# State-space mixer with outputs made as [feature, token] and the norm's scale applied behind the out-projection

## The chip, the cores and the metric

The kernel runs on 1 of the 8 cores of one Trainium2 chip. Its engines work side by side, each on its own queue: TensorE (PE, with its weight loads as PEld), VectorE (DVE), ScalarE (ACT), GpSimd (POOL) and SyncE (SP), which issues most DMAs. The metric is the device time of one execution in microseconds (us), as the median of several runs.

## What is computed

A two-layer decoder trunk on 512 tokens of 1024 features in float32. Layer 0 mixes with attention, layer 1 with a state-space mixer; each layer is `x <- LN(alpha*x + mixer(x))`, then a feed-forward part with a norm of its own and a gated embedding. Only the mixer of layer 1 changes:

```python
def ssd_mixer(x, w_in, conv_w, conv_b, dt_bias, a_log, d_skip, norm_w, w_out):
    h = x @ w_in
    z, xbc, dt = split(h)                       # 2048, 3072, 32
    xbc = silu(causal_depthwise_conv(xbc))      # 4 taps
    xs, bm, cm = split(xbc)                     # 32 heads of 64; 4 groups of B and C, 128 states
    dt = softplus(dt + dt_bias); a = -exp(a_log)
    y = ssd_chunked_scan(xs, dt, a, bm, cm)     # chunks of 128 tokens:
    #   la = cumsum(dt*a);  xdt = xs*dt
    #   y  = (cb * exp(la_i - la_j), j <= i) @ xdt         "intra"
    #   y += (C @ state) * exp(la_i)                       "inter"
    #   state = state*exp(la_end) + B^T (exp(la_end - la) * xdt)
    y = y + d_skip*xs
    y = y * silu(z)
    y = y * rsqrt(mean(y*y over the group's 512 features) + eps) * norm_w
    return y @ w_out
```

## The kernel before, in words

Products of large operands are made of three matmuls each (`mm3`, L104 to L107): an operand is split into a high and a low part in fp32r (`split`, L71: ACT writes the high part at L73, DVE the low one at L76; weights with a gain go through L98 and L99), and high x high, high x low and low x high are added up in PSUM. Weight tiles come by DMA from SP's queue into `raw`, are split into the 10 tiles of `wp`, and so run ahead of PE. The small products of the scan are plain float32 matmuls; each shows in the trace as two matmul instructions.

`ssd` (L755) works group by group: 4 groups `g` of 8 heads (512 features), 4 chunks `c` of 128 tokens. `Inputs(g).part(0..3)` makes the group's inputs: part 0 B and C (`conv_in`: projection as [feature, token], convolution, SiLU; then `bk` turns B on PE), parts 1 and 2 the 512 features of x, two blocks of 128 each, turned to [token, feature] on PE (`xf`, L969, evacuated by ACT at L970), part 3 the gate z as [token, feature] (`proj_b`: four accumulators side by side, evacuated at L976 and L977 into four tiles `z`). `Scan.chunk(c)` makes the state (L904), `intra` (L914: for each head the weights E, 128x128, with 64 moving columns), `inter` (L918: one matmul of 512 columns), adds them to `y = d_skip * xf` (POOL, L899; DVE, L915 to L921), multiplies with z (L924), takes the sum of squares (ACT, L927), `rsqrt` (DVE L126, POOL L127) and scales y (L929). `turn` transposes y on PE (L936) and splits it into `yT`. `mixer_out` multiplies yT with the out-projection, whose weights carry `norm_w` as gain, and adds to the residual stream `xs` (L203, L205).

The loop at L986 runs the scan of group g with the parts of group g+1 and the out-projection of group g-1 between its chunks; the last group has no inputs to make, and `mixer_last` follows it with the layer norm. The order within each engine's queue is not written out here: a planner builds it from a simulated timeline, in which program order is the priority and the buffers of each pool (`one`, `two`, `three`, `four`, `zp`, `cvp`, `yp`: the number is that of their buffers) hold an instruction back until a tile is free. Each engine then runs its queue strictly in that order.

In the attention part, `values` (L363, L368) makes products with 64 columns of weights for two heads in turn, whose results go to partitions 0 to 63 and 64 to 127 of one accumulator; the change uses that form.

Of the kernel before, what the change touches and what calls it, by code (L numbers as in the profile page):

```python
# [33 lines left out]
def trunk(ctx, tc, I, out):  # L34
# [720 lines left out]
    def ssd(xs, xT):  # L755
        with ExitStack() as es:
# [7 lines left out]
            zp = lpool("zp", 4)  # L764
            cvp = lpool("cvp", 2)
            yp = lpool("yp", 3)
# [4 lines left out]
            gn = one.tile([P, 16], F32, name="gn")  # L771
            nc.scalar.dma_start(gn, I["ssd_norm"])
            hv = one.tile([P, 3, 32], F32, name="hv")
            nc.scalar.dma_start(hv, I["ssd_heads"].partition_broadcast(P))
            dtb, alog, dsk = hv[:, 0], hv[:, 1], hv[:, 2]
# [53 lines left out]
            ones = scr("ones")  # L829
            G.memset(ones[:, :P], 1.0)  # L830
            b2 = bank("le")
            T.matmul(b2[:, :P], ones[:, :P], da, start=True, stop=True)
            ela, eend, elast = (one.tile([P, P], F32, name=n) for n in ("ela", "eend", "elast"))
            A.activation(ela, la, AF.Exp)
# [3 lines left out]
            rows = dp.tile([P, P], F32, name="rows")  # L838
            nc.scalar.dma_start(rows, lt)

# [10 lines left out]
            def run_out(g, yT, w, half, t):  # L851
                ps = acc()
                for k in range(4):
                    step_b(ps, (yT[:, 0, k], yT[:, 1, k]), w[k], t, 512, k == 0, k == 3)
                residual(xs[t], half, ps, ALPHA if g == 0 else None)

            def mixer_out(g, yT, half):
                w = load_out(g, half)
                for t in range(NT):
                    run_out(g, yT, w, half, t)  # L860

            def mixer_last(g, yT, w, ln, new, t):
                for half in range(2):
                    run_out(g, yT, w[half], half, t)
                    ln.stats(t, xs[t], half)
                ln.finish(t, xs[t], new)

            class Scan:
                def __init__(self, g, BT, CT, Bk, xf, z):
                    self.g, self.BT, self.CT, self.Bk, self.xf, self.z = g, BT, CT, Bk, xf, z  # L870
                    self.yT = two.tile([P, 2, 4, 512], F32R, tag="yT", name="yT")
                    self.state, self.y = None, []

                def weights(self, c):
                    g = self.g
                    ts = slice(c * P, (c + 1) * P)
                    hs = slice(c * 32 + g * 8, c * 32 + g * 8 + 8)
                    E = three.tile([P, 8, P], F32, tag="lab", name="lab")
                    nc.scalar.dma_start(E.rearrange("p h i -> p (h i)"),
                                        rows[hs, :].rearrange("h i -> (h i)").partition_broadcast(P))  # L880
                    b = bank("cb")
                    T.matmul(b[:, :P], self.BT[:, ts], self.CT[:, ts], start=True, stop=True)
                    cb = st.tile([P, P], F32, tag="cb", name="cb", bufs=2)
                    V.tensor_tensor(cb, b[:, :P], tri, op=OP.mult)
# [5 lines left out]
                    G.tensor_tensor(d8(xdt), d8(self.xf[:, c]), h8(dt[:, hs]), op=OP.mult)  # L890
                    self.E, self.xdt = E, xdt

                def chunk(self, c):
                    g, xf, state = self.g, self.xf[:, c], self.state
# [3 lines left out]
                    y = yp.tile([P, 512], F32, tag="y", name="y")  # L898
# [31 lines left out]
                    self.y.append(y)  # L930

                def turn(self, c):
                    ts = slice(c * P, (c + 1) * P)
                    b = bank("yT")
                    for k in range(4):
                        T.transpose(b[:, k * P:(k + 1) * P], self.y[c][:, k * P:(k + 1) * P], ident)  # L936
                    split(self.yT[:, 0, :, ts], self.yT[:, 1, :, ts], b.rearrange("p (k m) -> p k m", m=P))
# [9 lines left out]
            class Inputs:  # L947
                def __init__(self, g):
                    self.g = g
                    self.BT, self.CT = (four.tile([P, 512], F32, tag="BC", name=n) for n in ("BT", "CT"))  # L950
                    self.Bk = two.tile([P, 512], F32, tag="Bk", name="Bk")
                    self.xf = two.tile([P, NT, 512], F32, tag="xf", name="xf")
                    self.z = []

                def part(self, i):
# [8 lines left out]
                    elif i < 3:  # L964
                        for k in (2 * i - 2, 2 * i - 1):
                            f = conv_in(4 * g + k, None)
                            b = bank("xf")
                            for c in range(NT):
                                T.transpose(b[:, c * P:(c + 1) * P], f[:, c * P:(c + 1) * P], ident)  # L969
                            A.activation(self.xf[:, :, k * P:(k + 1) * P], b.rearrange("p (c m) -> p c m", m=P),  # L970
                                         AF.Copy)
                    else:
                        def evac(t, ps):
                            y = zp.tile([P, 512], F32, tag="z", name="z")

                            A.activation(y, ps, AF.Tanh, scale=0.5)  # L976
                            V.scalar_tensor_tensor(y, y, 1.0, ps, op0=OP.add, op1=OP.mult)  # L977
                            self.z.append(y)

                        proj_b(k_of(xT), I["w_z"][g], 512, evac)  # L980
# [5 lines left out]
            for g in range(4):  # L986
                sc = Scan(g, ins.BT, ins.CT, ins.Bk, ins.xf, ins.z)
# [16 lines left out]
            for t in range(NT):  # L1004
                if not t:
                    sc.turn(NT - 1)
                mixer_last(3, sc.yT, w, ln, new, t)
# [21 lines left out]
def layout(a):  # L1029
# [21 lines left out]
    o["w_z"] = _rows_by_pair(w[:, :2048])  # L1051
# [4 lines left out]
    o["ssd_heads"] = np.concatenate([f["ssd_dt_bias"], f["ssd_a_log"], f["ssd_d"]])  # L1056
    o["ssd_norm"] = f["ssd_norm"][0].reshape(16, P).T
# [26 lines left out]
```

## Time and profile before

| | us |
|---|---|
| median of 3 runs | 1474.02 (1474.0 to 1474.66) |
| the profiled execution | 1475.73 |
| its span, first to last instruction | 1473.9 |
| the mixer's stretch in it | about 668 to 1066 |

The profile is of one execution. Its span is the time from the first to the last instruction; 1.8 us of the execution lie around it. A row of instruction groups gives line, engine, operation, out<-in, shapes and count, then the busy time, the mean duration in ns of one, and the engine's idle time before. Busy times of PE are modelled from starts, so on PE the distance of two starts is the better price. The chain of work is followed back from the last instruction, and each piece of it is time that set the end.

### The profile page before, as it was taken

To read this page: it belongs to the slowest core of one execution; us is meant where nothing else is said; L and a number is where in the kernel's file an instruction comes from. 1 tells how busy PE (TensorE), PEld (TensorE's weight loads), DVE (VectorE), ACT (ScalarE), POOL (GpSimd) and SP (SyncE) were. 2 spreads that over 40 slices of the span, in tenths; PEclk is the share of its full clock that TensorE was granted. 3 is DMA by queue.
4 is the path that set the end of the run, shared out by engine and by line. 5 is a ranking of instruction groups with operands and counts; after the bars stand their busy time and mean duration, and the time that the engine had idled before them with its cause. 6 is when DMAs were issued, how large, how long until landed. Compare 5 with 4: busy or idle time off the path is not lost.

```text
span 1473.9 us, 18843 instructions
## 1 busy us (share of the span) xinstructions
PE 1458.1 (99%) x7128; PEld 1207.7 (82%) x7128; DVE 851.6 (58%) x1465; ACT 644.9 (44%) x1225; POOL 165.3 (11%) x261
## 2 busy tenths in 40 slices
PE   9998999999999999999999999999999999999998
PEld 7875878988888888889888888888888888888887
DVE  5266886554554324756576776758954445433382
ACT  5476653534343323334655554553253434422331
POOL 2134313000000000100222221122100000000010
PEclk9999999999999999999999999999999999999999
DMA  6304142233332334332433333333233333323411
GB/s 234 111 29 154 58 145 75 88 98 101 100 99 88 100 100 134 139 103 79 129 113 93 108 100 100 101 100 102 100 109 92 100 100 94 96 97 100 158 57 57
DMA packets 45259, 152.71 MB, mean 104 GB/s; under 512 B 6000, under 2 KB 6640, under 8 KB 45168
## 3 DMA queue, kind: packets, MB, share of 16 engines
q1 hardware_dynamic: 39168, 135.49, 28.7%
q10 hardware_dynamic: 6000, 16.01, 3.2%
q8 instruction: 56, 0.92, 0.2%
q14 instruction: 35, 0.29, 0.1%
HBM read 145.12 MB, written 5.31 MB: 102 GB/s over the span
## 4 chain that ended last, share of the span: by engine, by line
PE 93%; issue 3%; DVE 2%; ACT 1%; POOL 1%; DMA 1%; ACTq 0%; DVEq 0%; POOLq 0%
PE acc L106 24%; PE acc L107 24%; PE acc L105 24%; PE pg L106 2%; PE pg L105 2%; PE pg L107 2%; PE intra L914 2%; PE s L329 1%; PE xTb L136 1%; PE pt L356 1%; PE o L368 1%; PE inter L918 1%; PE state L904 1%; DVE w L76 1%; PE om L105 1%
## 5 line engine op out<-in xcount | busy, mean ns | idle before, releaser
L76 DVE TENSOR_TENSOR w<-raw,w 128x512 fp32r<-128x512 f32 (+1 forms) x438 | 300.9, 698 | 274.4 <-ACT w L73 273.9
L73 ACT ACTIVATE w<-raw 128x512 fp32r<-128x512 f32 (+1 forms) x438 | 268.4, 626 | 419.4 <-PE acc L107 371.2
L105 PE MATMUL acc<-xTh,w 128*128 128x512 f32 (+1 forms) x976 | 363.4, 374 | 0.4 <-ACT xTh L73 0.4
L106 PE MATMUL acc<-xTl,w 128*128 128x512 f32 (+1 forms) x976 | 362.8, 372 | 0.2 <-DVE xTl L76 0.2
L107 PE MATMUL acc<-xTh,w 128*128 128x512 f32 (+1 forms) x976 | 362.8, 372 | 0.0
L106 PEld LDWEIGHTS acc<-xTl,w 128*128 128x128 f32 x976 | 183.9, 188 | 32.5 <-issue 0.7
L105 PEld LDWEIGHTS acc<-xTh,w 128*128 128x128 f32 x976 | 183.1, 188 | 32.8 <-issue 0.7
L107 PEld LDWEIGHTS acc<-xTh,w 128*128 128x128 f32 x976 | 183.8, 188 | 31.8
L106 PE MATMUL acc<-w,h 128*128 128x512 f32 x352 | 137.1, 390 | 0.0
L107 PE MATMUL acc<-w,h 128*128 128x512 f32 x352 | 136.8, 390 | 0.0
L105 PE MATMUL acc<-w,h 128*128 128x512 f32 x352 | 136.6, 389 | 0.0
L604 DVE SCALAR_TENSOR_TENSOR conv<-acc,cw,conv 128x511 f32<-128x511 f32 x88 | 65.7, 746 | 87.5 <-ACT conv L602 87.5
L127 POOL TENSOR_TENSOR mv<-rs,half_neg 128x1 f32<-128x1 f32 x16 | 13.4, 843 | 761.6 <-DVE rs L126 761.6
L106 PE MATMUL acc<-w,xTh 128*128 128x512 f32 x224 | 86.9, 390 | 0.0
L105 PE MATMUL acc<-w,xTh 128*128 128x512 f32 x224 | 86.8, 394 | 0.0
L107 PE MATMUL acc<-w,xTl 128*128 128x512 f32 x224 | 86.5, 392 | 0.0
L105 PEld LDWEIGHTS acc<-w,h 128*128 128x128 f32 x352 | 66.1, 188 | 13.7
L106 PEld LDWEIGHTS acc<-w,h 128*128 128x128 f32 x352 | 66.1, 188 | 13.7
L107 PEld LDWEIGHTS acc<-w,h 128*128 128x128 f32 x352 | 66.1, 188 | 13.6
L602 ACT ACTIVATE conv<-acc,cw 128x512 f32<-128x512 f32 x44 | 34.3, 780 | 83.9 <-PE acc L107 83.9
L604 DVE SCALAR_TENSOR_TENSOR cv<-acc,scw,cv 128x511 f32<-128x511 f32 (+2 forms) x72 | 53.4, 744 | 23.7 <-ACT cv L602 23.2
L628 DVE TENSOR_TENSOR conv<-conv,acc 128x512 f32<-128x512 f32 x44 | 30.3, 688 | 60.1 <-PE acc L107 57.6
(278 smaller groups left out, 2197.2 us busy)
## 6 DMA issues: line engine op xcount, KB each, us to landing
raw<-in_w_up SPq DMA_DIRECT2D x88, 512.0 KB, 3.5
raw<-in_w_down SPq DMA_DIRECT2D x44, 512.0 KB, 3.5
raw<-in_w_xbc SPq DMA_DIRECT2D x24, 512.0 KB, 3.5
raw<-in_w_ple_gate SPq DMA_DIRECT2D x16, 512.0 KB, 4.9
raw<-in_w_z SPq DMA_DIRECT2D x16, 512.0 KB, 3.6
lab<-rows ACTq DMA_DIRECT2D x16, 512.0 KB, 4.4
raw<-in_w_sout SPq DMA_DIRECT2D x16, 512.0 KB, 3.5
raw<-in_w_qkv SPq DMA_DIRECT2D x11, 512.0 KB, 4.6
```

The costliest lines, as they stand in the source:

```text
L73: A.activation(h, src, AF.Copy)
L76: eng.tensor_tensor(l, src, h.bitcast(F32), op=OP.subtract)
L105: T.matmul(ps, lh, rh, start=start, stop=False)
L106: T.matmul(ps, lh, rl, start=False, stop=False)
L107: T.matmul(ps, ll, rh, start=False, stop=stop)
L136: T.transpose(b[:, k * P:(k + 1) * P], src[:, (half * 4 + k) * P:(half * 4 + k + 1) * P], ident)
L329: T.matmul(b[:, :e], q[:, ts], k[:, :e], start=n == 0, stop=n == len(qk) - 1)
L356: T.transpose(b[:, at:at + P], self.soft[x][2][i][:, t], ident)
L602: A.activation(f, ps, AF.Identity, bias=cw[:, taps:taps + 1], scale=cw[:, taps - 1:taps])
L604: V.scalar_tensor_tensor(f[:, k:], ps[:, :S - k], cw[:, taps - 1 - k:taps - k], f[:, k:], op0=OP.mult, op1=OP.add)
L628: V.tensor_tensor(g, g, pu, op=OP.mult)
L914: T.matmul(b[:, s], E[:, h], xdt[:, s], start=True, stop=True)
```

## The change

The scan's outputs are made as [feature, token]: in `pairs`, the weights are 64 columns of xdt (or of the state) for one head, the moving operand is E (or C) with 128 columns, and the results of heads 2k and 2k+1 go to partitions 0 to 63 and 64 to 127. `turn` and its transposes go. The decay exp(la) of `inter` now varies along the free dimension: `erows` is written to DRAM once and comes back broadcast over partitions as `el`, by two DMAs for each chunk but the first, on ACT's queue. `d_skip * x` is made by ACT from the convolution's output (`xd`), in halves of 256 tokens, as are the evacuations of `xf`. z is projected as [feature, token] into one tile with a single buffer. The sum of squares goes over partitions: squares (ACT), a sum over the 4 feature blocks (`tensor_reduce`, DVE), and a matmul with a column of ones (`ss`). The norm's factor `rs` is applied to the accumulator of the out-projection while it is added to `xs`, which has been multiplied by alpha beforehand on ACT. Both halves of the out-projection of the group before now stand behind chunks 0 and 1.

```diff
@@ pools
-            zp = lpool("zp", 4)
+            zp = lpool("zp", 1)
-            yp = lpool("yp", 3)
...
@@ before the loop
-            A.activation(ela, la, AF.Exp)
...
+            elt = scr("elt")[:, :P]
+            A.activation(elt, lt, AF.Exp)
+            nc.scalar.dma_start(erows, elt)
+            for t in range(NT):
+                A.activation(xs[t], xs[t], AF.Copy, scale=ALPHA)
@@ run_out
-                residual(xs[t], half, ps, ALPHA if g == 0 else None)
+                s = slice(half * 512, (half + 1) * 512)
+                V.scalar_tensor_tensor(xs[t][:, s], ps, sc.rs[:, t:t + 1], xs[t][:, s], op0=OP.mult, op1=OP.add)
@@ Scan
+                def pairs(self, b, weights, moving):
+                    for k in range(4):
+                        for x in range(2):
+                            h = 2 * k + x
+                            T.matmul(b[64 * x:64 * x + 64, k * P:(k + 1) * P], weights[:, h * 64:h * 64 + 64], moving(h),
+                                     start=True, stop=True)
@@ chunk
-                    G.tensor_tensor(d8(y), d8(xf), h8(dsk[:, g * 8:g * 8 + 8]), op=OP.mult)
+                    if c:
+                        el = two.tile([P, 4, P], F32, tag="el", name="el")
+                        for x in range(2):
+                            src = erows[hs, :].rearrange("(k x) i -> x k i", x=2)[x]
+                            nc.scalar.dma_start(el[64 * x:64 * x + 64], src.partition_broadcast(64))
...
+                    y = two.tile([P, 4, P], F32, tag="y", name="y")
                     b = bank("intra")
-                    for h in range(8):
-                        s = slice(h * 64, h * 64 + 64)
-                        T.matmul(b[:, s], E[:, h], xdt[:, s], start=True, stop=True)
-                    V.tensor_tensor(y, y, b, op=OP.add)
+                    self.pairs(b, xdt, lambda h: E[:, h])
+                    b = b.rearrange("p (k i) -> p k i", i=P)
                     if c:
-                        b = bank("inter")
-                        T.matmul(b, self.CT[:, ts], state, start=True, stop=True)
-                        t_ = scr("yi")
-                        V.tensor_tensor(d8(t_), d8(b), h8(ela[:, hs]), op=OP.mult)
-                        V.tensor_tensor(y, y, t_, op=OP.add)
+                        bi = bank("inter")
+                        self.pairs(bi, state, lambda h: self.CT[:, ts])
+                        V.tensor_tensor(y, bi.rearrange("p (k i) -> p k i", i=P), el, op=OP.mult)
+                        V.tensor_tensor(y, y, b, op=OP.add)
+                        V.tensor_tensor(y, y, xd[:, :, hc], op=OP.add)
+                    else:
+                        V.tensor_tensor(y, b, xd[:, :, hc], op=OP.add)
                     if c < NT - 1:
                         self.weights(c + 1)
-                    V.tensor_tensor(y, y, self.z[c], op=OP.mult)
-                    ss = st.tile([P, 2], F32, tag="gs", name="gs")
-                    junk = scr("junk")
-                    A.activation(junk, y, AF.Square, accum_out=ss[:, 0:1])
-                    rsqrt(ss[:, 1:2], ss[:, 0:1], 0.25 / 512, RMS_EPS)
-                    V.tensor_scalar(y, y, ss[:, 1:2], 0.5, op0=OP.mult, op1=OP.mult)
...
-                        T.transpose(b[:, k * P:(k + 1) * P], self.y[c][:, k * P:(k + 1) * P], ident)
-                    split(self.yT[:, 0, :, ts], self.yT[:, 1, :, ts], b.rearrange("p (k m) -> p k m", m=P))
+                    V.tensor_tensor(y, y, self.z[:, :, ts], op=OP.mult)
+                    if half == 0:
+                        self.yT.append(three.tile([P, 2, 4, 256], F32R, tag="yT", name="yT"))
+                    split(self.yT[-1][:, 0, :, hc], self.yT[-1][:, 1, :, hc], y)
+                    sq = scr("sq").rearrange("p (k i) -> p k i", i=P)
+                    A.activation(sq, y, AF.Square)
+                    s1 = st.tile([P, P], F32, tag="s1", name="s1", bufs=2)
+                    V.tensor_reduce(s1, sq.rearrange("p k i -> p i k"), axis=mybir.AxisListType.X, op=OP.add)
+                    b = bank("ss")
+                    T.matmul(b[:, :1], s1, ones[:, :1], start=True, stop=True)
+                    rsqrt(self.rs[:, c:c + 1], b[:, :1], 1.0 / 512, 4 * RMS_EPS)
@@ Inputs.part: xf (now three half tiles of 256 tokens) and xd (the same)
-                            A.activation(self.xf[:, :, k * P:(k + 1) * P], b.rearrange("p (c m) -> p c m", m=P),
-                                         AF.Copy)
+                            for h in range(2):
+                                A.activation(self.xf[h][:, :, k * P:(k + 1) * P], b[:, 2 * h:2 * h + 2], AF.Copy)
+                                A.activation(self.xd[h][:, k], f[:, h * 256:(h + 1) * 256], AF.Copy,
+                                             scale=dsk[:, 4 * g + k:4 * g + k + 1])
@@ Inputs.part: z
-                        proj_b(k_of(xT), I["w_z"][g], 512, evac)
+                        self.z = zp.tile([P, 4, 512], F32, tag="z", name="z")
+                        for k in range(4):
+                            ps, = up_a([load_w(I["w_z"][4 * g + k])], xT, False)
+                            A.activation(self.z[:, k], ps, AF.Tanh, scale=0.5)
+                            V.scalar_tensor_tensor(self.z[:, k], self.z[:, k], 1.0, ps, op0=OP.add, op1=OP.mult)
@@ the loop
-                    if c:
-                        sc.turn(c - 1)
-                    elif prev:
-                        prev.turn(NT - 1)
...
-                    if prev and c in (0, 2):
-                        mixer_out(g - 1, prev.yT, c // 2)
+                    if prev and c < 2:
+                        mixer_out(prev, c)
```

## Rows read from the trace of the kernel before

**Rows 1.** The page: busy time, share and instructions per engine; the chain's shares.
```profile
PE 1458.1 (99%) x7128; PEld 1207.7 (82%) x7128; DVE 851.6 (58%) x1465; ACT 644.9 (44%) x1225; POOL 165.3 (11%) x261
PE 93%; issue 3%; DVE 2%; ACT 1%; POOL 1%; DMA 1%; ACTq 0%; DVEq 0%; POOLq 0%
```
**Rows 2.** Windows of the mixer: length, busy PE, PEld, DVE, ACT, POOL, clock, DMA.
```profile
668.00:730.00 62.00, 62.00 (x353) 54.27 (x352) 38.20 (x70) 37.76 (x76) 4.16 (x4) 1.00 0.37 118
730.00:1000.00 270.00, 269.52 (x1314) 220.11 (x1313) 193.10 (x293) 142.96 (x290) 62.82 (x55) 1.00 0.31 101
1000.00:1066.00 66.00, 66.00 (x378) 55.87 (x378) 59.37 (x101) 21.65 (x43) 13.02 (x14) 1.00 0.31 105
```
**Rows 3.** Chain of work, in order of time (start, us, what), from two stretches.
```profile
727.08 3.90 POOL y L899 x3
730.98 1.01 POOL xe L902
...
751.35 0.86 PE state L904 x2
752.21 1.73 PE intra L914 x16
753.94 0.91 PE inter L918 x2
...
756.69 0.44 PE yT L936 x4
```
**Rows 4.** Timeline of PE around a block of `values`: start, us, what.
```profile
173.86 0.39 PE L106 MATMUL wo<-w,ob 128*128 128x512 f32 x1
174.09 0.39 PE L107 MATMUL wo<-w,ob 128*128 128x512 f32 x1
174.41 2.37 PE L368 MATMUL o<-pt,v 128*64 128x512 f32 x16
176.71 0.50 PE L329 MATMUL s<-mk,mq 96*128 96x512 f32 x1
```
**Rows 5.** Line 368: durations of its matmuls and their forms.
```profile
L368 PE MATMUL o<-pt,v x128: 272/432/1116, 95.3 to 225.3; 128*64 128x512 f32 x32, 128*64 128x384 f32 x32, 128*64 128x256 f32 x32, 128*64 128x128 f32 x32
```
**Rows 6.** Timeline of PE: float32 matmuls with 32 moving columns.
```profile
679.92 1.07 PE L795 MATMUL dt<-raw,dtT 64*128 64x32 f32 x8
680.92 0.39 PE L105 MATMUL acc<-xTh,w 128*128 128x256 f32 x1
```
**Rows 7.** Groups of DVE and POOL in 660 to 1070 us.
```profile
L929 DVE TENSOR_SCALAR y<-y,gs 128x512 f32<-128x512 f32 x16 | 8.1, 504 | 4.5 <-POOL gs L127 4.4
L76 DVE TENSOR_TENSOR yT<-yT 128x512 fp32r<-128x512 f32 x16 | 10.9, 680 | 1.4 <-ACT yT L73 1.4
L888 DVE TENSOR_TENSOR lab<-lab,cb 128x1024 f32<-128x1024 f32 x16 | 23.8, 1486 | 0.0
L197 DVE SCALAR_TENSOR_TENSOR x<-lnt,mv,lnlab 128x512 f32<-128x512 f32 x8 | 5.7, 746 | 0.0
L899 POOL TENSOR_TENSOR y<-xf,hv 128x512 f32<-128x512 f32 x16 | 20.9, 1311 | 0.7 <-PE yT L936 0.7
```
**Rows 8.** Groups of ACT in the same stretch.
```profile
L970 ACT ACTIVATE xf<-xf 128x512 f32<-128x512 f32 x16 | 9.5, 594 | 6.7 <-PE xf L969 6.6
L98 ACT ACTIVATE w<-raw,gn 128x512 fp32r<-128x512 f32 x32 | 22.8, 719 | 16.3 <-PE acc L107 16.2
L887 ACT ACTIVATE lab<-lab 128x1024 f32<-128x1024 f32 x16 | 16.8, 1050 | 0.0
```
**Rows 9.** Timelines of POOL and DVE in the last group.
```profile
1002.08 1.49 POOL L899 TENSOR_TENSOR y<-xf,hv 128x512 f32<-128x512 f32 x1
1002.59 2.07 DVE L888 TENSOR_TENSOR lab<-lab,cb 128x1024 f32<-128x1024 f32 x1
1025.78 1.22 DVE L888 TENSOR_TENSOR lab<-lab,cb 128x1024 f32<-128x1024 f32 x1
```
**Rows 10.** DMA issues: what, queue, count, KB each, us to landing.
```profile
lab<-rows ACTq DMA_DIRECT2D x16, 512.0 KB, 4.4
```

More of the change, by code (lines that the diff above doesn't have):

```diff
@@ L770, in ssd @@
             V.tensor_scalar(cw, cw, 0.5, None, op0=OP.mult)
-            gn = one.tile([P, 16], F32, name="gn")
+            gn = one.tile([P, 32], F32, name="gn")
             nc.scalar.dma_start(gn, I["ssd_norm"])
-            hv = one.tile([P, 3, 32], F32, name="hv")
+            gn, dsk = gn[:, :16], gn[:, 16:]
+            hv = one.tile([P, 2, 32], F32, name="hv")
             nc.scalar.dma_start(hv, I["ssd_heads"].partition_broadcast(P))
-            dtb, alog, dsk = hv[:, 0], hv[:, 1], hv[:, 2]
+            dtb, alog = hv[:, 0], hv[:, 1]
             raw = rawp.tile([P, 1024], F32, tag="raw", name="raw")
@@ L828, in ssd @@
             V.tensor_copy(lt, b[:, P:2 * P])
-            ones = scr("ones")
-            G.memset(ones[:, :P], 1.0)
+            ones = one.tile([P, P], F32, name="ones")
+            G.memset(ones, 1.0)
             b2 = bank("le")
-            T.matmul(b2[:, :P], ones[:, :P], da, start=True, stop=True)
-            ela, eend, elast = (one.tile([P, P], F32, name=n) for n in ("ela", "eend", "elast"))
-            A.activation(ela, la, AF.Exp)
+            T.matmul(b2[:, :P], ones, da, start=True, stop=True)
+            eend, elast = (one.tile([P, P], F32, name=n) for n in ("eend", "elast"))
             A.activation(elast, b2[:, :P], AF.Exp)
@@ L837, in ssd @@
             A.activation(eend, eend, AF.Exp)
-            rows = dp.tile([P, P], F32, name="rows")
+            rows, erows = (dp.tile([P, P], F32, name=n) for n in ("rows", "erows"))
             nc.scalar.dma_start(rows, lt)
+            elt = scr("elt")[:, :P]
[3 more added lines that the diff above has]
+                A.activation(xs[t], xs[t], AF.Copy, scale=ALPHA)
             def h8(x):
@@ L849, in load_out, with run_out, mixer_out, mixer_last @@
                 return [w for u in range(2) for w in load_w(I["w_sout"][half, 2 * g + u], gain=gains[2 * u:2 * u + 2])]
[L851 removed]
+            def run_out(sc, w, half, t):
                 ps = acc()
                 for k in range(4):
[L854 to L858 removed]
+                    y = sc.yT[t // 2]
+                    step_b(ps, (y[:, 0, k], y[:, 1, k]), w[k], t % 2, 512, k == 0, k == 3)
+                s = slice(half * 512, (half + 1) * 512)
+                V.scalar_tensor_tensor(xs[t][:, s], ps, sc.rs[:, t:t + 1], xs[t][:, s], op0=OP.mult, op1=OP.add)
+            def mixer_out(sc, half):
+                w = load_out(sc.g, half)
                 for t in range(NT):
[L860 to L862 removed]
+                    run_out(sc, w, half, t)
+            def mixer_last(sc, w, ln, new, t):
                 for half in range(2):
[L864 removed]
+                    run_out(sc, w[half], half, t)
                     ln.stats(t, xs[t], half)
@@ L868, in ssd, with __init__ @@
             class Scan:
[L869 to L872, printed above, removed]
+                def __init__(self, i):
+                    self.g, self.BT, self.CT, self.Bk, self.xf, self.xd, self.z = i.g, i.BT, i.CT, i.Bk, i.xf, i.xd, i.z
+                    self.yT = []
+                    self.rs = st.tile([P, NT], F32, tag="rsg", name="rsg")
+                    self.state = None
                 def weights(self, c):
@@ L951, in __init__ @@
                     self.Bk = two.tile([P, 512], F32, tag="Bk", name="Bk")
-                    self.xf = two.tile([P, NT, 512], F32, tag="xf", name="xf")
-                    self.z = []
+                    self.xf, self.xd = [], []
+                    self.z = None
                 def part(self, i):
@@ L964, in part @@
                     elif i < 3:
+                        if i == 1:
+                            for h in range(2):
+                                self.xf.append(three.tile([P, 2, 512], F32, tag="xf", name="xf"))
+                                self.xd.append(three.tile([P, 4, 256], F32, tag="xd", name="xd"))
                         for k in (2 * i - 2, 2 * i - 1):
@@ L969, in part @@
                                 T.transpose(b[:, c * P:(c + 1) * P], f[:, c * P:(c + 1) * P], ident)
-                            A.activation(self.xf[:, :, k * P:(k + 1) * P], b.rearrange("p (c m) -> p c m", m=P),
-                                         AF.Copy)
-                    else:
[L973 to L978, printed above, removed]
-                        proj_b(k_of(xT), I["w_z"][g], 512, evac)
+                            b = b.rearrange("p (c m) -> p c m", m=P)
+                            for h in range(2):
+                                A.activation(self.xf[h][:, :, k * P:(k + 1) * P], b[:, 2 * h:2 * h + 2], AF.Copy)
+                                A.activation(self.xd[h][:, k], f[:, h * 256:(h + 1) * 256], AF.Copy,
+                                             scale=dsk[:, 4 * g + k:4 * g + k + 1])
+                    else:
+                        self.z = zp.tile([P, 4, 512], F32, tag="z", name="z")
[3 more added lines that the diff above has]
+                            V.scalar_tensor_tensor(self.z[:, k], self.z[:, k], 1.0, ps, op0=OP.add, op1=OP.mult)
             ins = Inputs(0)
@@ L1004, in ssd @@
             for t in range(NT):
-                if not t:
-                    sc.turn(NT - 1)
-                mixer_last(3, sc.yT, w, ln, new, t)
+                mixer_last(sc, w, ln, new, t)
         return new
@@ L1050, in layout @@
     w = f["ssd_w_in"][0]
-    o["w_z"] = _rows_by_pair(w[:, :2048])
+    o["w_z"] = _cols_by_feature(w[:, :2048])
     o["w_xbc"] = _cols_by_feature(w[:, 2048:5120])
```

18 lines of the change are left out of this document (7 added, 11 removed).

## The prediction, made before the changed kernel was run

> **What bounds the kernel now.** I read the page first: which engine is busy nearly all the time, and whether the chain of work that set the end runs through it. PE is busy for 1458 of 1474 us, and 93% of the chain is PE [rows 1]. A busy PE could still be a PE that waits between starts, so I looked at the stretch of the mixer by windows: PE is busy in 397.5 of 398 us there, at the full granted clock, while DVE is at 0.73, ACT at 0.51 and POOL at 0.20 [rows 2]. The chain in that stretch runs from matmul to matmul: projections with the scan's blocks between them, and one stop at 727 to 732 us, where PE's first state matmul waits for three `y` and one `xe` on POOL [rows 3]. So in the mixer a microsecond of PE work is a microsecond of the kernel, both ways, as long as DVE and ACT keep up; the third window is where that is least sure, since DVE is at 59.4 of 66 us in it [rows 2].
>
> The profiled execution took 1475.7 us with a span of 1473.9; the median is 1474.0. I sum against the profiled one and move the sum to the median.
>
> **PE, part by part.** *The transposes of y* (4 for each of 16 chunks): 0.44 us a chunk on the chain [rows 3], so 16 x 0.44 = 7.0 us go, with nothing in their place.
>
> *intra and inter.* Before, intra takes 1.73 us a chunk: 16 instructions of 64 moving columns. The state's two passes over 512 columns take 0.86 us, which is 0.84 ns a column and pass [rows 3]; 16 x 64 columns would be 0.86 us at that rate, so half of intra is weight loading that the short moving operand doesn't cover. inter takes 0.91 us in 12 chunks [rows 3]. After the change each has 8 weights of 64 columns, two passes, 128 moving columns: 2048 columns, 1.72 us at that rate, if they go one after another, and 0.86 us if the two heads of a pair run at once on the two column halves. The trace has that very form in the attention's `values`: 128x64 weights, alternating halves, moving 512, 384, 256 and 128 columns [rows 5]. A block of it holds 2 x 2 x (512+384+256+128) = 5120 columns, 4.30 us one after another, 2.15 in pairs; from its first start to the next matmul's start it takes 176.71 - 174.41 = 2.30 us [rows 4]. So the pairs run at once, with 0.15 us on top; and the matmul ahead of the block, whose like starts the next after 0.23 us, is followed after 0.32, another 0.09 [rows 4]. I charge 0.24 us for going into and out of the halves. Then a block of intra and inter costs 1.72 + 0.24 = 1.96 us instead of 2.64, 12 times: -8.2 us; intra alone 0.86 + 0.24 = 1.10 instead of 1.73, 4 times: -2.5 us. If the planner puts other matmuls between intra and inter, the 0.24 is due 12 times more, +2.9 us.
>
> The Trainium skill (TensorEngine Tiling (Array Packing), Key Properties) says that changing the tiling mode drains the engine, which speaks against short blocks in halves among full-width work. The 0.24 us agrees with it. Were there no such cost, the two terms would be 16 x 0.24 = 3.8 us larger.
>
> *ss.* 16 new matmuls of one moving column, two instructions each. The nearest row has 32 columns: 8 instructions in 1.00 us, ends included [rows 6], 0.125 each; I take 0.25 us a chunk, +4.0 us. At the far ends this is 0 (hidden in a weight load) or twice as much.
>
> *z* as [feature, token] has the same 96 matmuls of 512 columns a group. The projections, the state, cb and the turning of x and B stay. No change.
>
> PE's sum: -7.0 - 8.2 - 2.5 + 4.0 = -13.7 us.
>
> **Other engines, and what is late next.** *POOL* loses `y` = 16 x 1.31 = 21 us [rows 7]. That takes away the 3.9 us ahead of the first `xe`, and with it PE's half microsecond of idle time in the second window [rows 2, 3]: -0.5 us.
>
> *DVE.* Each chunk loses the scaling (0.50 us) and gets a sum over 4 strided blocks of 512 elements; nothing of that form is in the trace, and between 0.50 (one input, 512) and 1.49 (1024 elements) [rows 7] I take 0.69, near the many one-pass operations of 512 elements. The low half of yT now has both inputs in SBUF, 0.75 instead of 0.68; the additions stay three (two in the first chunk). So +0.26 x 16 = 4.2 us (1.1 to 17). The out-projection's addition gets a scale by pointer: 32 x (0.75 - 0.68) = 2.2 us at most [rows 7]. Against it stands that the E product took 2.07 us beside a POOL `y` and 1.22 without [rows 9]; over 16 of them the mean of 1.49 leaves 4 us that a quieter POOL may give back. DVE's load hardly changes: 0.73 to about 0.76 of a shorter stretch. The Trainium skill (VectorE: DVE Perf Modes, Rules for kernel authors) calls tensor_reduce the slowest DVE operation and advises against it on a hot path; in the unscaled mode that it names, 512 elements in fp32 would cost what the additions do, so the rule changes the sum only if strides cost extra, which is the upper bound above.
>
> *ACT.* xf's evacuation, 0.59 us, becomes two halves and two of xd: 4 instructions of 256 columns. Bounds for one: 0.30 (half of 0.59) and 0.72 (512 columns with a scale by pointer) [rows 8]; I take 0.5 with the fixed share counted in full: 16 x (2.0 - 0.59) = +23 us (10 to 37). The scaling of xs: 4 x 1.05 = 4.2 us [rows 8]. ACT goes from 202 to about 228 of 385 us, 0.59. This is hidden by the weight tiles that are split ahead: one load of two tiles feeds 24 matmuls, 24 x 0.23 = 5.5 us of PE, and there are ten tiles, so PE has up to 27 us in hand. In the first window ACT is at 37.8 of 62 us [rows 2] and gets about 6 + 4.2 us more there: full, but not over. If that cover is gone, up to 5 us of it show.
>
> *DMA.* `el` comes by 24 more DMAs of 128 KB on ACT's queue, behind whatever ACT waits for; the 512 KB broadcast `lab` lands after 4.4 us [rows 10], so I bound one by 0 and 4.4 us. The data are in DRAM from the start and there are two buffers, so it can be issued a chunk (some 20 us) ahead: nothing. Uncovered, DVE waits in front of the inter product, and 12 x 4.4 us = 53 us of DVE's idle 107 would be used, with the weight splits queued behind it.
>
> *Waits that are new.* z has one buffer: the tanh of the next group's z waits on ACT for the y*z of chunk 3, with weight splits behind it. y*z comes about 3 us after intra (four DVE operations), the first z accumulator is full 5.5 us after its start, behind intra in program order; covered by 2 us. The second half tiles of xf and xd wait for chunk 1, the second yT of a group for the out-projection at chunks 0 and 1; both stand earlier in program order, and PE has 22 us of other work there. I cost them at nothing.
>
> *The last group.* No inputs are left to fill PE, and with DVE at 0.90 [rows 2] the layer norm's chain is late next. Its share of PE's gain is 4 x 0.9 = 3.6 us; I count half of it as lost, +1.8 us (0 to 3.6).
>
> Sum: -13.7 - 0.5 + 1.8 = -12.4 us: the profiled execution goes to 1463.3, the median to 1461.6.
>
> **The rivals.**
> 1. *More is gained* (up to -19 us, 1455): the switches into the halves are hidden or ss costs nothing, and the last group keeps its gain. For: weight loads overlap elsewhere. Against: the 0.24 us is in the row for this very form.
> 2. *Partly eaten* (-3 to -8 us, 1466 to 1471): intra and inter are torn apart (+2.9), ACT is late in the first group (up to 5), the last group gives all of its 3.6 back. Each has a price; two of them together make this case.
> 3. *No change that shows* (within 2.9 us, or 0.2%, which is about what a measurement of this kernel can tell): all three of them.
> 4. *Slower, because the heads of a pair do not run at once.* The place is the pairs' matmuls, whose two heads the planner may part or whose operands arrive apart. Fully one by one, a block of intra and inter costs 3.44 + 0.24 = 3.68 us (+1.04, 12 times), intra alone 1.96 (+0.23, 4 times): +13.4 - 7.0 + 4.0 = +10.4, or 1484. Pairs and singles differ by 24 us in all, so it decides from about half of the pairs on. Against: in rows 4 all eight ran at once.
> 5. *Slower, because z's single buffer stops ACT.* Three times, at the change of groups, chunk 3's tail is later than the first z accumulator; each microsecond that it is late beyond the 2 us of cover holds PE through the accumulators and the weight splits. It outweighs the gain from 4.1 us each time; at 5.5, one z product, it is +16.5 - 12.4 = +4 us, 1478. For: the planner's times are not the chip's. Against: PE waits for nothing of the kind now [rows 2].
>
> **How the numbers follow.** Forecast (-8 to -15 us) 0.50; rival 1 0.13; rival 2 0.15; rival 3 0.07; rival 4 0.06; rival 5 0.09. Faster 0.78, same 0.07, slower 0.15. The predicted time is the forecast's, 1461.6. The range takes the forecast, rivals 1 and 2 and the near end of rival 3: 1455 to 1472, about 0.8.
>
> **What would show it.** Of the changed kernel: intra and inter together at about 1.96 us a chunk from start to the next start, with two starts some ns apart for each pair; no yT on PE; ss at 0.2 to 0.3 us; PE still busy in all but a few us of the mixer, which is about 12 us shorter; PE's gaps, if any, at the last norm. The forecast is wrong if PE's idle time in the mixer grows beyond 5 us (then rivals 2, 3 or 5, and the wait names which), or if the starts of a pair lie 0.1 us apart (rival 4).

## The result: slower, with PE standing still where it never had

The changed kernel takes 1484.97 us (1482.34 to 1487.44, 4 runs) against 1474.04 before; the ratio is 1.0073, 95% interval 1.0054 to 1.0092. The forecast was 1461.6 with a range up to 1472. The runs of the changed kernel lie 5 us apart; those of before lay 0.7 us apart here and about 4 us in the experiments below. The profiled execution is the slowest of the four, 1487.4 us.

The page of the changed kernel, busy time and chain:

```profile
PE 1456.1 (98%) x7264; PEld 1199.8 (81%) x7264; DVE 851.5 (57%) x1465; ACT 658.7 (44%) x1261; POOL 142.1 (10%) x245
PE 94%; DVE 3%; ACT 1%; DMA 1%; issue 1%; POOL 0%; ACTq 0%; DVEq 0%; POOLq 0%
```

The page hardly shows it: DVE is as busy as before and PE 2 us less [rows 1]. The windows of the mixer do (us, busy PE, PEld, DVE, ACT, POOL, granted clock, DMA):

```profile
668.00:730.00 62.00, 61.99 (x352) 53.98 (x351) 38.34 (x71) 41.07 (x86) 0.00 (x0) 1.00 0.41 123
730.00:800.00 70.00, 70.00 (x402) 56.15 (x401) 52.73 (x79) 42.28 (x91) 16.34 (x15) 1.00 0.37 120
800.00:820.00 20.00, 14.63 (x66) 10.90 (x65) 10.70 (x19) 9.92 (x21) 4.26 (x4) 0.83 0.17 46
820.00:1000.00 180.00, 180.00 (x968) 145.38 (x966) 129.49 (x197) 101.22 (x209) 26.89 (x26) 1.00 0.36 114
1040.00:1066.00 26.00, 17.14 (x86) 12.99 (x85) 22.71 (x40) 8.25 (x14) 3.10 (x5) 0.80 0.42 124
```

Before, PE stood for 0.5 us in the whole stretch, at full clock [rows 2]. Now it stands for 5.4 us in one window and 8.9 in another, and in both the granted clock is lower: 0.83 and 0.80, which is the lower level, 1.2 GHz, for 6.8 us and 10.2 us of them. In the other windows PE is busy throughout. PE's three longest waits in the mixer:

```profile
PE ss L957 <- DVE s L955: 5.4, 1, 5.4
PE xTb L136 <- DVE x L197: 4.0, 1, 4.0
PE acc L105 <- ACT yT L73: 3.8, 1, 3.8
```

The first stop on PE's timeline (start, us, what, idle time before):

```profile
801.34 0.39 PE L107 MATMUL acc<-xTh,w 128*128 128x512 f32 x1
807.10 0.56 PE L957 MATMUL ss<-ones,s 128*128 128x1 f32 x2 [5.37 <-DVE s L955]
...
810.65 0.63 PE L107 MATMUL acc<-xTh,w 128*128 128x512 f32 x1
811.08 0.63 PE L105 MATMUL acc<-xTh,w 128*128 128x512 f32 x1
...
812.17 0.40 PE L105 MATMUL acc<-xTh,w 128*128 128x512 f32 x1
812.40 0.40 PE L106 MATMUL acc<-xTl,w 128*128 128x512 f32 x1
```

PE stands in front of `ss`, the new matmul of one column, and behind the stop equal matmuls start 0.43 us apart instead of 0.23 until about 812 us. So this stop costs twice: its own length, and the slow stretch after it. What made `ss` late shows on ACT and DVE:

```profile
795.97 0.32 ACTq L890 DMA_DIRECT2D lab<-rows  x1
...
801.73 0.40 ACT L897 ACTIVATE lab<-lab,la 128x128 f32<-128x128 f32 x1 [6.02 <-PE acc L107]
802.04 2.14 ACT L897 ACTIVATE lab<-lab,la 128x128 f32<-128x128 f32 x7
804.60 0.61 ACT L73 ACTIVATE yT<-y 128x512 fp32r<-128x512 f32 x1
805.12 0.61 ACT L953 ACTIVATE sq<-y 128x512 f32<-128x512 f32 x1
...
800.06 0.69 DVE L948 TENSOR_TENSOR y<-y,z 128x512 f32<-128x512 f32 x1
805.93 1.02 DVE L955 TENSOR_REDUCE s<-sq 128x128 f32<-128x512 f32 x1
```

y was ready on DVE at 800.7 us. Its squares were made by ACT only at 805, because ACT had stood for 6.0 us in front of a Relu whose broadcast `lab` had been issued at 795.97. (The row names PE as the releaser, which had long been done; the trace's record of the DMA has it landing at 801.71, just ahead of the Relu.)

The second large stop, in the last group, on DVE and ACT:

```profile
1037.54 0.21 DVE L184 BATCH_NORM_AGGREGATE mv<-bn 128x2 f32<-128x12 f32 x1
1040.59 0.16 DVE L126 TENSOR_SCALAR rs<-ss 128x1 f32<-128x1 f32 x1 [2.84 <-PE ss L957]
1041.41 0.75 DVE L861 SCALAR_TENSOR_TENSOR x<-acc,rsg,x 128x512 f32<-128x512 f32 x1 [0.66 <-POOL rsg L127]
...
1046.69 0.63 ACT L73 ACTIVATE yT<-y 128x512 fp32r<-128x512 f32 x1 [12.89 <-DVE y L948]
```

DVE stands 2.8 us for `ss` of chunk 2, which PE has queued behind matmuls of the out-projection, then works its way to y of chunk 3; by then PE has nothing left but the product that needs that y, and stands 3.8 us. The third wait, 4.0 us at 1057 us for the layer norm's x, comes behind `ss` of chunk 3, which PE starts at 1056.5 us.

### The profile page after: what moved, and what is told of

It reads as the page before. It is cut to its first block, busy times and chain, and to the rows that moved or that the text cites. A ratio compares the mean times of both kernels' runs of the same rounds, so it can differ in the third digit from the quotient of the medians.

```text
span 1485.7 us, 19157 instructions
## 1 busy us (share of the span) xinstructions
PE 1456.1 (98%) x7264; PEld 1199.8 (81%) x7264; DVE 851.5 (57%) x1465; ACT 658.7 (44%) x1261; POOL 142.1 (10%) x245
## 4 chain that ended last, share of the span: by engine, by line
PE 94%; DVE 3%; ACT 1%; DMA 1%; issue 1%; POOL 0%; ACTq 0%; DVEq 0%; POOLq 0%
PE acc L105 25%; PE acc L107 25%; PE acc L106 25%; PE pg L105 2%; PE pg L106 2%; PE pg L107 2%; PE s L329 1%; PE intra L908 1%; PE xTb L136 1%; PE pt L356 1%; PE o L368 1%; PE state L927 1%; PE inter L908 1%; DVE w L76 1%; PE om L105 1%
## 5 line engine op out<-in xcount | busy, mean ns | idle before, releaser
L106 PE MATMUL acc<-xTl,w 128*128 128x512 f32 (+1 forms) x1104 | 414.4, 376 | 0.5 <-DVE xTl L76 0.5
L105 PE MATMUL acc<-xTh,w 128*128 128x512 f32 (+1 forms) x1104 | 414.4, 377 | 0.0
L107 PE MATMUL acc<-xTh,w 128*128 128x512 f32 (+1 forms) x1104 | 414.0, 375 | 0.0
L106 PEld LDWEIGHTS acc<-xTl,w 128*128 128x128 f32 x1104 | 208.2, 189 | 37.8 <-issue 1.0
L107 PEld LDWEIGHTS acc<-xTh,w 128*128 128x128 f32 x1104 | 208.2, 189 | 37.6 <-issue 0.9
L105 PEld LDWEIGHTS acc<-xTh,w 128*128 128x128 f32 x1104 | 207.7, 189 | 37.7 <-DVE z L1007 0.5
L106 PEld LDWEIGHTS acc<-w,h 128*128 128x128 f32 x352 | 66.1, 188 | 13.7
L105 PE MATMUL acc<-w,yT 128*128 128x512 f32 x128 | 52.9, 413 | 3.8 <-ACT yT L73 3.8
L107 PE MATMUL acc<-w,yT 128*128 128x512 f32 x128 | 52.2, 410 | 0.6 <-DVE yT L76 0.6
L106 PE MATMUL acc<-w,yT 128*128 128x512 f32 x128 | 51.9, 405 | 0.0
```

What stands on the lines that cost most here:

```text
L105: T.matmul(ps, lh, rh, start=start, stop=False)
L106: T.matmul(ps, lh, rl, start=False, stop=False)
L107: T.matmul(ps, ll, rh, start=False, stop=stop)
```

## The experiments

Each stands beside runs of the kernel before on the same chip, whose median was between 1473.99 and 1474.10 us.

**Undo the halves.** `e4_one_half`: in `pairs`,

```diff
-                    for k in range(4):
-                        for x in range(2):
+                    for x in range(2):
+                        for k in range(4):
```

> The changed kernel with the loops of the pairs turned round: first the four even heads (partitions 0 to 63), then the four odd ones (64 to 127), so that neighbours in PE's queue use the same column half. If the gain of intra and inter comes from two heads at once, the blocks of 16 go from 0.92 to 1.02 us to about 1.8 to 1.95 us each, 28 blocks, and the kernel gets some 20 to 25 us longer where PE is the bound (1500 to 1510 us). If the narrow weights alone make them cheap, the blocks stay at 1 us and the time within the spread of 1482 to 1487 us.

1492.85 us, ratio 1.0126 (1.0106 to 1.0146), between the two expectations. The blocks went from 1.02 to 1.51 us, not to 1.8, and the time went up by 8 us. By their starts, the first odd heads run beside the last even ones, so that part of the overlap survives; whether the planner or the engine puts them side by side, no run tells. With stops around, I couldn't tell price from cover, so the same edit was made again in a kernel without stops (`e12_all_one_half`, below).

**ss one chunk later.** `e1_ss_late`: the matmul and rsqrt in a method of their own, called where `turn` was.

```diff
+                def total(self, c):
                     b = bank("ss")
...
                     sc.chunk(c)
+                    if c:
+                        sc.total(c - 1)
+                    elif prev:
+                        prev.total(NT - 1)
...
```

> The changed kernel with one thing moved: the matmul ss and its rsqrt are issued one chunk later, where the kernel before had its transposes of y (same work, same buffers). Theory A (PE's queue is strictly in order; ss stands in it at the place of its own chunk, behind a chain ACT lab, ACT sq, DVE s, and PE stands still when that chain is late): the gap of 5.4 us ahead of ss at 807 us goes, with the half-speed stretch behind it (about 2 us), and DVE's wait of 2.8 us for ss in the last group: 1472 to 1478 us. Theory B (the single buffer of z is what stops PE: all four accumulators hold z until chunk 3 has used the old one): the gap stays at the same place, ahead of another matmul: 1482 to 1487 us. Theory C (the order of the last group is the larger part): little moves at 807 us, the gaps at 1043 and 1057 us stay: 1478 to 1485 us.

1476.02 us, ratio to before 1.0012 (1.0003 to 1.0021): 9 us of the loss go when two instructions move to another place in PE's queue. The stop in front of ss is gone, and DVE no longer waits for it in the last group. What PE waits for now:

```profile
PE intra L908 <- DVE lab L899: 3.4, 1, 3.4
PE xTb L136 <- DVE xTl L76: 2.7, 1, 2.7
PE xTb L136 <- DVE x L197: 1.7, 2, 1.1
```

Theory A holds, but at the same change of groups PE now stands in front of intra. ACT had stood 4.7 us for `lab`, as before, so that its splits came late; DVE stood for one of these, and the product that completes E came late behind it:

```profile
799.99 0.69 DVE L76 TENSOR_TENSOR w<-raw,w 128x512 fp32r<-128x512 f32 x1 [3.45 <-ACT w L73]
...
802.05 1.21 DVE L899 TENSOR_TENSOR lab<-lab,cb 128x1024 f32<-128x1024 f32 x1
```

**The same fault put into the kernel before.** `b1_turn_now`: `sc.turn(c)` right behind `sc.chunk(c)`, not one chunk later.

> The kernel before with one thing moved: the transposes of y are issued in their own chunk, not one chunk later. Theory A (matmuls at the end of a chunk's chain stop PE when they are not put off): PE gets gaps of several us ahead of yT at group changes, 1480 to 1490 us. Theory B (z's buffer) and theory C (order of the last group): within 3 us of 1474.

1478.44 us, ratio 1.0030 (1.0019 to 1.0041), with two stops of PE in front of `yT`, 2.0 us together, and a stretch at half clock in the last group. The sign is theory A's; the stops are not the several us each that it expected, and the time lies below its lower end of 1480.

**z's single buffer put into the kernel before.** `b2_z_one`: the four z tiles become one `[P, NT, 512]` tile with one buffer.

> The kernel before with one thing changed: the four tiles of z become one tile with a single buffer, as in the changed kernel, so that z of the next group waits for chunk 3. Theory B: PE gets gaps at the group changes, 3 to 6 us each at one or more of three, with half speed behind them: 1479 to 1492 us. Theories A and C: within 3 us of 1474.

1474.31 us, ratio 1.0003 (0.9993 to 1.0012). No stop but those of the kernel before, 0.6 us at most. Theory B falls for that kernel. A second buffer for z in the changed kernel was not tried; but e8 to e10 below keep the single one, and PE stops for 0.6 us or not at all at a change of groups in them.

**lab one chunk earlier.** `e5_fetch` (in the changed kernel) and `e6_late_fetch` (with ss late): the DMA moved out of `weights` into a function called two chunks ahead.

> The changed kernel with the broadcast lab issued one chunk earlier (same DMAs, same three buffers, ss in its own chunk). At 796 to 802 us ACT stood 6 us for lab, and the split of yT, the squares and with them DVE's sum and PE's ss stood behind it. Theory A1 (the late DMA on ACT's queue is what makes the chain to ss late): the 5.4 us gap at 807 us and the half speed behind it go, the last group stays: 1476 to 1479 us. Theory A2 (the chain to ss is late anyway; its place in PE's queue is the fault): the gap stays, 1482 to 1487 us.

> The kernel with ss one chunk later, and lab issued one chunk earlier as well. There, PE still stood 4.0 us at 799 us for intra, whose E waited on ACT for lab (4.7 us). Theory A1: that gap and about 1.7 us of half speed go: 1469 to 1472 us, with the last group as the rest. If the gap is PE running out of other work at that change of groups, it stays: 1474 to 1477 us.

1482.98 us (1.0059, 1.0044 to 1.0074) and 1476.0 us (1.0011, 1.0002 to 1.0021): e5's 2.0 us lie within the spread of the runs, e6 gains nothing, and both stops are there (4.2 and 3.3 us), as theory A2 and the second case of e6 have it. I had misread the issue: it was not late. `lab` has three buffers, and each issue stands right behind the intra that frees one, in every kernel here. By the order of the issues, the Relu on which ACT stood at 796 to 802 us was that of the third chunk ahead (the expectation of e8 says the chunk after next), whose product DVE starts only at 841 us: work that nobody needed yet, put early into a queue that runs strictly in order.

**Hold that Relu back.** `e8_relu` (changed kernel), `e9_late_relu` (with ss late), `b4_relu` (kernel before): Relu and Exp of chunk n are queued on ACT behind the squares of chunk n-2.

```diff
-                    for h in range(8):
-                        A.activation(E[:, h], E[:, h], AF.Relu, bias=la[:, hs][:, h:h + 1], scale=-1.0)
-                    A.activation(E, E, AF.Exp, scale=-1.0)
+                    n = 4 * g + c
+                    with tc.issue_after(sqs[n - 2].ins) if n > 1 else ExitStack():
+                        ...
```

> The changed kernel with one edge of order more: on ACT, the Relu and Exp of chunk n's E stand behind the squares of chunk n-2. (The broadcast lab was issued as soon as its buffer was free already, three chunks ahead, so that issuing it earlier could not help; the planner puts the Relu of the chunk after next into ACT's queue 1.5 us behind that issue, the data land 3.6 to 5.7 us behind it, and ACT stands for work that nobody needs yet, with the weight splits and the split of yT behind it.) Theory A3 (this stop of ACT is what makes PE stand at 807 us): the 5.4 us gap and its half speed go, the last group stays: 1474 to 1479 us. If ss in its own chunk stops PE anyway: 1481 to 1487 us.

> The same edge in the kernel with ss one chunk later. Theory A3: the 4.0 us gap at 799 us goes with about 1.7 us of half speed: 1469 to 1472 us, and what is left against the forecast of 1461.6 is the last group. If the gap stays: 1474 to 1478 us.

> The kernel before with the same edge of order on ACT. ACT's waits for lab (21 us in all) shrink, but PE never stood for them there, since the transposes come a chunk later: 1473 to 1475 us. If it gains more than 3 us, the waits cost the kernel before as well.

1478.77 us (1.0033, 1.0019 to 1.0048), 1470.47 us (0.9981, 0.9971 to 0.9991) and 1473.37 us (0.9997, 0.9987 to 1.0006). All three as theory A3 has it. The Relu waits for `lab` for at most 1.6 us in all in any of them (21 us in the kernel before), which gives 6.2 us in the changed kernel and nothing that can be told in the one before, whose PE had work in hand while ACT stood. In e8 ss stands in place and costs 0.6 us at the change of groups; the stops of the last group are as in the changed kernel. What is left in e9 is the last group alone:

```profile
PE xTb L136 <- DVE x L197: 3.5, 1, 3.5
PE xTb L136 <- DVE xTl L76: 1.9, 1, 1.9
```

**Take work from DVE in the last group.** First by the norm: `e7_late_shared` (with ss late) and `b3_shared` (kernel before) call `ln.finish(t, xs[t], new, True)`.

> The kernel with ss one chunk later, and the last norm of the mixer in the form that the attention's norm uses: ACT applies mean and scale, DVE multiplies with the gain, POOL adds the bias (DVE loses 8 of 16 operations of 0.65 us, 5.3 us; ACT gets 8, POOL 8). Theory C (in the last group DVE is the bound of the changed kernel: 62 of 68 us busy there, 10.0 of 10 at 1040 to 1050 us): 4 to 8 us are gained, 1468 to 1472 us. If the last group is bound by the chain of chunks or by PE's order, DVE's relief gains under 2 us: 1474 to 1477 us.

> The kernel before with the same form of the last norm. Theory C says that the kernel before is bound by PE there (66 of 66 us busy) with DVE just below: no change, 1473 to 1475 us, or slower by the longer way through ACT and POOL at the very end. If it gains 3 us or more as well, DVE bound the last group before the change too.

1479.59 us (1.0040, 1.0026 to 1.0054) and 1478.43 us (1.0027, 1.0017 to 1.0036): slower by about 4 us both. Both of e7's expectations missed, and it tells nothing on DVE's load: the bias on POOL stands in the chain of each token block, and in e7 PE waits 4.0 us for it. Then without a longer chain: `e10_late_relu_sum` is e9 with the sum over the four feature blocks made by PE in the last group (the lines are those of e11),

```diff
-                    V.tensor_reduce(s1, sq.rearrange("p k i -> p i k"), axis=mybir.AxisListType.X, op=OP.add)
+                    if g < 3:
+                        V.tensor_reduce(s1, ...)
+                        sq = s1[:, None, :]
...
-                    T.matmul(b[:, :1], s1, ones[:, :1], start=True, stop=True)
+                    for k in range(n):
+                        T.matmul(b[:, :1], sq[:, k], ones[:, :1], start=k == 0, stop=k == n - 1)
```

and `e11_sum` is the changed kernel with this edit alone.

> As e9, and in the last group alone the sum over the four feature blocks is made by PE (four accumulating matmuls with the squares as weights and the column of ones) instead of DVE: DVE loses 4 x 1.05 us, PE gets 12 more matmuls, about 2.6 us. Theory C (DVE is the bound of the last group, 62 of 68 us busy): 3 to 5 us faster than e9. If PE or the chain of chunks is the bound there: 0 to 3 us slower than e9.

> The changed kernel with the last edit alone: in the last group PE makes the sum of squares over the feature blocks, DVE no longer; ss stays in its own chunk and ACT's order as it is. If DVE's work is what makes the last group of the changed kernel long whatever else is wrong, 3 to 6 us are gained: 1479 to 1482 us. If there it is the round trip through ss (DVE waits 2.8 us for PE, then PE 3.8 us for the split of yT), the edit gains under 3 us as long as ss stays in place: 1482 to 1486 us.

e10: 1464.97 us, ratio to before 0.9937 (0.9923 to 0.9952), 5.5 us better than e9, a little above the expected 3 to 5, although PE got 12 more matmuls. In e9 DVE is busy for all of the 20 us in which PE stands for 6.0:

```profile
1030.00:1050.00 20.00, 14.01 (x67) 11.11 (x66) 20.00 (x39) 7.82 (x13) 3.05 (x4) 0.89 0.34 106
```

So DVE bounds the last group once the stops ahead of it are gone. e11: 1481.8 us (1.0052, 1.0035 to 1.0068), 3.2 us below the changed kernel, which the spread of the runs does not separate from nothing and which lies at the border of the two expectations; the share of DVE's work in the changed kernel itself stays open. Windows of e10 and its only wait above half a microsecond:

```profile
730.00:986.00 256.00, 256.00 (x1394) 206.34 (x1392) 195.75 (x288) 148.96 (x313) 47.20 (x43) 1.00 0.37 115
986.00:1052.00 66.00, 64.30 (x416) 53.38 (x416) 57.65 (x99) 24.22 (x49) 12.11 (x13) 1.00 0.34 109
```
```profile
PE acc L106 <- DVE xTl L76: 1.7, 1, 1.7
```

Full clock, PE busy to 1.7 us, and no slow stretch behind this stop: this is the state that I had forecast for the changed kernel, and with 1465.0 us it beats both kernels.

**Undo the halves where PE never stops.** `e12_all_one_half`: e10 with the loops of `pairs` turned round.

> The fastest version so far (ss one chunk later, the edge of order on ACT, the last group's sum on PE; 1465.0 us, PE idle for under 2 us in the mixer) with the loops of the pairs turned round, four even heads and then four odd ones. In the changed kernel that made the blocks 1.51 instead of 1.02 us but cost only 8 us, with PE's stops around it. Where PE never stops, 28 blocks x 0.5 us have to show in full: 12 to 15 us, 1477 to 1480 us. If it is again about 8 us or less, part of the price is hidden by something that is not in the account: 1470 to 1474 us.

1474.36 us, 9.4 us more than e10. The chain of e12, and of e10 at the same chunk:

```profile
752.04 1.18 PE intra L912 x13
753.22 0.06 PE inter L912
753.28 0.05 PE intra L912
753.33 0.06 PE inter L912
...
753.55 0.99 PE inter L912 x13
```
```profile
748.98 1.02 PE intra L912 x16
750.00 0.87 PE inter L912 x16
```

2.50 us for the two blocks against 1.89. The last odd heads of intra run beside the first even ones of inter, as the two halves do within a block, so my 12 to 15 us were too many; but the distances of starts over all blocks of intra and inter sum to 36.3 us in e12 and 27.0 in e10, 9.3 us more, and the time grew by 9.4. The price of the halves is on the path, and this account closes.

## Why the prediction was wrong, step by step

**PE's terms held, to 2.3 us of 13.7.** The blocks of intra and inter in the changed kernel, and ss, on its chain:

```profile
774.73 0.12 PE ss L957 x2
...
778.99 1.02 PE intra L908 x16
780.02 0.87 PE inter L908 x16
```

1.89 us together, forecast 1.96; the two are torn apart in 3 of 12 chunks, which costs 0.15 us each. Summed over starts, intra and inter fell by 10.1 us (forecast 10.7), the transposes by 5.8 (7.0), ss came to 2.6 (4.0), and 1.9 us more stand at the matmuls just ahead of the blocks (state, xf; by e9, which has no stop there), where I had put the way into the halves. That is 11.4 us less work on PE; I had 13.7. A matmul of the projections ahead of a block is followed after 0.32 us instead of 0.23, and a block of 16 takes 1.02 us, 0.15 more than its eight pairs at 0.109: the sizes that the attention's rows gave. The Trainium skill (TensorEngine Tiling (Array Packing), Key Properties) says that a change of the tiling mode drains the engine, and these extra times agree with it.

The measured time is within 1 us of rival 4's 1484, by chance: its heads one by one would make the two blocks 3.68 us, and they take 1.89. The prediction's own sign of being wrong did appear, PE's idle time of more than 5 us in the mixer, but the wait, `ss`, is in none of the rivals that it points to.

**The step that failed is "Waits that are new ... I cost them at nothing".** The list had z, xf, xd and yT on it and not the one that counted. I priced ss as 0.25 us of PE and never asked where it stands in PE's queue and behind which chain: ACT's squares, DVE's sum, and all that ACT and DVE have queued ahead of these. The transposes that it replaces hung on a chain as long, but the loop put them off by one chunk, some 25 us; the diff shows that this went, and I read it as pure removal ("go, with nothing in their place"). e1 and b1 show the effect in both directions: 9.0 us gained, 4.4 lost.

**"ACT ... is hidden by the weight tiles that are split ahead"** was right on ACT's load (214.6 us in the stretch, I had 228) and wrong on its order. ACT's standing for `lab` is in the trace of before, and there the cover hid it (b4: no gain). With ss and E close to it the cover was gone, as my sentence on the price "if that cover is gone, up to 5 us" had it; the price was 6.2 us (e8). Rival 5 had the place, the mechanism (a wait on ACT at a change of groups, with splits behind it) and the length of a stop (5.5 us, measured 5.4, but once and not three times), but hung it on z's buffer, which costs nothing (b2, e9, e10). `el`, which I costed at nothing, did cost nothing: its DMAs land after 5.0 us in the median, above my bound of 4.4, and no product on DVE waits for one.

**The price of a stop was too small.** The trace of before has no stop of PE above 0.5 us in the mixer, and I summed stops at their length. Here 13.9 us more of idle time came with 14.4 us of PE's work at the lower clock, 7.2 us lost on top. Then -11.4 + 13.9 + 7.2 = +9.7 us, against +10.9 between the first `dt` matmul and the last matmul of the kernel; the rest, 1.2 us, stays open.

**The last group** was mis-sized, and most of the loss stands there. I counted half of PE's gain of 3.6 us there as lost, so that the forecast is -10.6 us up to the last group and -1.8 in it. Two starts split the time in each trace, the first `dt` matmul and the first intra of the last group:

| profiled execution, us | `dt` to last group | from there to the last matmul |
|---|---|---|
| before | 332.2 | 470.9 |
| changed kernel | 331.3 | 482.6 |
| e8 (Relu held back) | 323.4 | 482.7 |
| e9 (and ss late) | 322.1 | 477.4 |
| e10 (and sum on PE) | 322.1 | 472.5 |

Up to the last group the changed kernel is 0.8 us ahead in spite of its stop, and without it 10.1 ahead (e9), which is the forecast. Then it loses 11.8 us. Of these, 5.3 go with ss one chunk later and 4.9 with DVE's sum; the Relu has no part in them. The sum:

```profile
L955 DVE TENSOR_REDUCE s<-sq 128x128 f32<-128x512 f32 x16 | 17.2, 1073 | 0.0
```

1.07 us, where I took 0.69 from bounds of 0.50 and 1.49. Whether the strides or the operation cost extra, no run tells. The Trainium skill (VectorE: DVE Perf Modes, Rules for kernel authors) warns of this operation on a hot path, and the 1.07 us against the 0.69 of y times z, both of 512 elements, agrees. The low half of yT, which I put at 0.75, stayed at 0.68. POOL's relief gave as much back: DVE's busy time is the same as before in all, the E product fell from 1.49 to 1.25 us, and the four of the last group from 7.3 to 4.9 us together. So DVE's load there stays about the same (4.3 us of sums more, 2.2 of scaling and 2.4 of E products less). It was nearly full already [rows 2], and taking this sum away is worth 5.5 us once the stops are gone (e10 against e9).

Undone one after another, from 1485.0: ACT's Relu 6.2, ss one chunk later 8.3, DVE's sum in the last group 5.5, which makes 1465.0, within the forecast's own case (1459 to 1466), though by a kernel with three more edits. The chance of 0.09 for a loss through a stopped ACT was the only part of the 0.15 for slower that this was.

## What to carry to other kernels

When an edit puts a matmul at the end of a chain through other engines, price its place in PE's queue and not its length: ask what PE has in hand if the chain is late, and put it off by as long as its result can wait. A wait of an in-order engine that costs nothing in one profile is hidden by work that another engine has in hand; look who will stand behind it after the edit. On a kernel whose PE never stops, price a stop of some us at its length plus the half-speed stretch that stood behind such stops here.

## What was unexpected of the hardware

A matmul with one moving column and 128x128 float32 weights takes 0.14 us from its start to the next start for both its instructions (0.12 on the chain), little more than half of the 0.25 that the rows with 32 columns made me charge [rows 6]. Four heads on one column half followed by four on the other still overlap in part: 1.51 us for a block of 16, where one by one would be about 1.9 (16 at 0.109, and 0.15). In alternation, the two heads of a pair start 0.007 us apart and the next pair 0.103 us later. And 256 columns cost ACT 0.38 us from PSUM and 0.50 from SBUF with a scale by pointer, so that two copies of a half take 0.76 us where one of the whole took 0.59 [rows 8]:

```profile
L999 ACT ACTIVATE xd<-cv,gn 128x256 f32<-128x256 f32 x32 | 14.4, 501 | 9.6 <-DVE cv L966 9.5
L998 ACT ACTIVATE xf<-xf 128x256 f32<-128x256 f32 x32 | 10.3, 379 | 5.9 <-PE xf L995 5.9
```
